# Sixty-six small transfers of a decoder step's output stage issued from GpSimd in place of SyncE

## The chip, the core and the metric

The kernel runs on one core of one Trainium2 chip. The metric is the time of one execution in device microseconds, as the median of several runs. A core has five engines with an instruction queue each: TensorE (PE in the profile, with its weight loads as PEld), VectorE (DVE), ScalarE (ACT), GpSimd (POOL) and SyncE (SP). Each works through its queue in order and waits on semaphores. SyncE computes nothing here; it only issues transfers. GpSimd computes and can issue transfers too. The transfers themselves run on 16 DMA engines that all queues share.

## What is computed

One inference step of one layer, for a prompt of 256 tokens and a sample of 8 sequences with 4 new tokens each (32 rows), with a width of 2048:

```
proj = x @ w_in                                  # 288 rows in all
y_r, s_T, new_shift = rwkv_time_mix(proj[..., :RWKV_COLS], ...)     # 16 heads, matrix state
y_n, ...            = nsa_mix(proj[..., RWKV_COLS:], ...)           # compressed, selected, window branch
h = concat([y_r, y_n]) @ w_out
x = layer_norm(ALPHA * x + h, ln1_g, ln1_b)
f = peer_ffn(x, ...)        # top-16 experts per head by product keys, rows of u and v gathered
x = layer_norm(ALPHA * x + f, ln2_g, ln2_b)
```

`new_shift` is the last projected row of the prompt and of each of the 8 sequences, 3360 columns each. The outputs are the two x, the new keys and values, the new states and these nine shift rows.

## The kernel before

The kernel is one long program written in stages; a scheduler puts the instructions of each engine in an order, by its own estimate of when each can start, among the instructions of several generators that are woven together. Which instruction stands where on an engine is therefore the scheduler's result, and a changed line can move others.

The stages in the order of time are: projection and recurrence of the prompt (up to line 1560), the sample's attention and recurrence (line 1578, `weave((late, 137), ...)`), the output stage (lines 1683 to 1688), layer norm 1 (lines 1695 to 1714), the product-key search (lines 1779 to 1805), the dense expert products (lines 1818 to 1845), and the sum over expert values with the last layer norm.

The change lies in the output stage. Three generators are woven there:

- `sample_chain` (line 1447) does the sample's 32 rows: it loads the gate weights (`gate_rows`, lines 1413 and 1414, into the ring `cw` of 5 buffers), multiplies (lines 1454 to 1456), and then forms the 32 rows times `w_out` in `product_rows`. Each of its 32 loads of 512 KB (line 1476, ring `cw`) feeds 4 matmuls (line 1478). `product_rows` takes them in two halves `h`, and four groups of four loads in a half; the first two groups multiply `YNs`, the others `BV`. After a group `put1` adds the sum on DVE: line 1486 for the first group of a half, which reads the input rows `xr_`, line 1488 for the others. Then come the norm with `gs_` and `bs_` (`norm_quarters`, lines 1436 and 1437), the same product with `peer_wq`, the choice of experts, and 64 gathers of rows of `peer_u` with a dot product each (lines 1533 and 1534).
- `prompt_attention` does the prompt's attention: lines 643 to 666 the compressed branch, lines 681 to 716 scores, exponentials, transposes (line 700) and value products (line 707).
- `out_first` (line 1660) transposes the shift rows (line 1666), copies them to the tile `SHR` (line 1667), stores them with 18 transfers (lines 1670 and 1671), computes the prompt's gate (lines 1677 to 1679, 8 pairs of matmuls from a second copy of the gate weights) and starts `out_part(0, BV)`: the prompt rows times the upper half of `w_out`, 16 loads of 512 KB (line 1642), each split into a rounded part on ACT (line 1644) and a rest on DVE or, for every fourth load, on GpSimd (line 1645), then 12 matmuls (line 1650). The buffers of line 1642 come from a ring `wraw` of 4, and `SHR` takes one of these four first, the gate weights two more.

The transfers that the change touches are those of lines 1464 and 1466 (in the generator `sample_chain`) and of lines 1670 and 1671. Lines 1464 and 1466 load `xr_` (for each half and quarter 4 loads of 8 rows by 256 columns, 32 in all) and `gs_` and `bs_` (8 loads each of one stretch of 256 numbers repeated over 32 rows). That is 32 + 16 + 18 = 66 transfers.

## Time and profile before

| | us |
|---|---|
| median of 3 runs | 2595.13 |
| lowest and highest of these | 2588.27 and 2599.22 |
| the profiled execution | 2602.22 |
| its span, first to last instruction | 2600.4 |
| PE busy / DVE busy / POOL busy in the span | 2328.9 / 1955.5 / 1281.1 |
| mean granted TensorE clock | 0.93 |

The profile is one execution. A row of its table of stretches gives for each engine the busy time and, after x, the number of instructions, then the granted clock of TensorE as a share of full speed (PEclk), then the share of the DMA engines that is busy and the rate. A row of its timeline gives the start, the time, the engine, the line, the operation, the tile written and the tiles read, a count, and in square brackets the idle time ahead of it with what ended it. SPq rows are the issues on SyncE's queue. A fp32 matmul shows as two records, a transpose as one, so that four matmuls of line 1478 are 8 records. In a timeline row that merges several records the time runs from the first start to the last end.

### The profile page before, as it was taken

To read this page: it belongs to the slowest core of one execution; us is meant where nothing else is said; L and a number is where in the kernel's file an instruction comes from. 1 tells how busy PE (TensorE), PEld (TensorE's weight loads), DVE (VectorE), ACT (ScalarE), POOL (GpSimd) and SP (SyncE) were. 2 spreads that over 40 slices of the span, in tenths; PEclk is the share of its full clock that TensorE was granted. 3 is DMA by queue.
4 is the path that set the end of the run, shared out by engine and by line. 5 is a ranking of instruction groups with operands and counts; after the bars stand their busy time and mean duration, and the time that the engine had idled before them with its cause. 6 is when DMAs were issued, how large, how long until landed. Compare 5 with 4: busy or idle time off the path is not lost.

```text
span 2600.4 us, 47649 instructions
## 1 busy us (share of the span) xinstructions
PE 2328.9 (90%) x17612; PEld 1961.5 (75%) x17612; DVE 1955.5 (75%) x4360; ACT 1027.7 (40%) x1932; POOL 1281.1 (49%) x1327
## 2 busy tenths in 40 slices
PE   7989999979989997469799999996699799989996
PEld 7877898865555655358699999995677688878885
DVE  4789756554742538949988888889976689878988
ACT  3433222224432332210244444443566544434443
POOL 5677423232510107635544444445555577767772
PEclk9989999988986997779899999997899999999998
DMA  7877964467656867886499999997778699899994
GB/s 222 241 218 241 275 199 139 130 200 223 213 178 234 275 243 245 312 267 172 153 371 349 352 352 346 352 338 225 232 241 294 233 324 326 319 336 322 325 322 174
DMA packets 346650, 683.49 MB, mean 263 GB/s; under 512 B 81338, under 2 KB 204785, under 8 KB 345361
## 3 DMA queue, kind: packets, MB, share of 16 engines
q1 hardware_dynamic: 251505, 344.67, 40.9%
q0 software_dynamic: 94912, 335.77, 36.9%
q8 instruction: 139, 2.28, 0.3%
q14 instruction: 94, 0.77, 0.1%
HBM read 664.77 MB, written 23.88 MB: 265 GB/s over the span
## 4 chain that ended last, share of the span: by engine, by line
PE 66%; DVE 17%; DMA 8%; issue 4%; POOL 3%; ACT 2%; SPq 0%; DVEq 0%; POOLq 0%; ACTq 0%
PE pb L2024 19%; PE ph L1832 14%; PE pj L417 6%; PE pt L1826 4%; DMA co<-in_cache_cmp_kv,gidx 2%; PE pj L1790 2%; PE pa L1650 2%; DVE rows L1756 2%; DVE CA L471 2%; PE ss L1478 2%; PE sa L918 1%; PE pa L1906 1%; PE p L1061 1%; PE px L1876 1%; PE fs L1924 1%
## 5 line engine op out<-in xcount | busy, mean ns | idle before, releaser
L448 POOL DMA_INDIRECT rq<-in_peer_v,gi x256 | 374.7, 1463 | 170.4 <-issue 80.7
L448 POOL DMA_INDIRECT rows<-in_peer_u,gi x256 | 298.6, 1166 | 313.3 <-DVE rows L1756 282.8
L1832 PE MATMUL ph<-XHd,ul 128*128 128x256 f32 x1024 | 304.6, 297 | 18.1 <-DVE ul L1622 18.1
L1756 DVE SCALAR_TENSOR_TENSOR rows<-rows,x1a 128x1024 f32<-128x1024 f32 x256 | 309.3, 1231 | 5.7 <-DMA rows<-in_peer_u,gi 5.5
L1832 PE MATMUL ph<-XHd,uh 128*128 128x256 f32 x1024 | 297.4, 290 | 0.3 <-ACT uh L1621 0.3
L1832 PE MATMUL ph<-XLd,uh 128*128 128x256 f32 x1024 | 290.7, 284 | 0.0
L1621 ACT CAST uh<-pt 128x512 fp32r<-128x512 f32 x256 | 149.8, 587 | 277.6 <-PE ph L1832 203.6
L417 PE MATMUL pj<-XH,wh 128*128 128x288 f32 (+1 forms) x752 | 230.4, 307 | 12.3 <-DVE ss L747 7.0
L417 PE MATMUL pj<-XH,wl 128*128 128x288 f32 (+1 forms) x752 | 232.2, 309 | 9.3 <-DVE wl L412 6.5
L1622 DVE TENSOR_TENSOR ul<-pt,uh 128x512 fp32r<-128x512 f32 x256 | 176.0, 689 | 80.8 <-ACT uh L1621 72.9
L417 PE MATMUL pj<-XL,wh 128*128 128x288 f32 (+1 forms) x752 | 226.7, 302 | 0.0
L2024 PE MATMUL pb<-vl,ah 128*128 128x512 f32 x768 | 217.7, 392 | 0.3 <-DVE vl L2018 0.3
L2024 PE MATMUL pb<-vh,al 128*128 128x512 f32 x768 | 216.4, 390 | 0.0
L2024 PE MATMUL pb<-vh,ah 128*128 128x512 f32 x768 | 199.1, 395 | 16.3 <-ACT vh L2017 16.3
L1832 PEld LDWEIGHTS ph<-XHd,ul 128*128 128x128 f32 x1024 | 196.7, 192 | 20.2 <-DVE ul L1622 20.0
L410 ACT CAST wh<-wraw 128x512 fp32r<-128x512 f32 (+1 forms) x188 | 114.8, 616 | 234.7 <-PE pj L417 180.2
L1832 PEld LDWEIGHTS ph<-XHd,uh 128*128 128x128 f32 x1024 | 197.3, 193 | 0.8 <-ACT uh L1621 0.5
L1832 PEld LDWEIGHTS ph<-XLd,uh 128*128 128x128 f32 x1024 | 197.0, 192 | 0.0
L1998 DVE SCALAR_TENSOR_TENSOR fP<-rq,ge,fP 128x512 f32<-128x512 f32 x254 | 189.9, 748 | 2.4
L2024 PEld LDWEIGHTS pb<-vh,ah 128*128 128x128 f32 x768 | 146.3, 191 | 47.7 <-ACT vh L2017 17.3
L471 DVE SCALAR_TENSOR_TENSOR CA<-co,wbc,CA 128x256 f32<-128x256 f32 x248 | 131.8, 570 | 55.8 <-DMA co<-in_cache_cmp_kv,gidx 55.6
L2024 PEld LDWEIGHTS pb<-vl,ah 128*128 128x128 f32 x768 | 145.8, 190 | 31.3 <-DVE vl L2018 0.7
(852 smaller groups left out, 5546.6 us busy)
## 6 DMA issues: line engine op xcount, KB each, us to landing
ur<-in_peer_u SPq DMA_DIRECT2D x128, 512.0 KB
wraw<-in_w_in SPq DMA_DIRECT2D x152, 256.0 KB
cw<-in_w_out SPq DMA_DIRECT2D x32, 512.0 KB
wraw<-in_w_out SPq DMA_DIRECT2D x32, 512.0 KB
cw<-in_peer_wq SPq DMA_DIRECT2D x32, 512.0 KB
wraw<-in_peer_wq SPq DMA_DIRECT2D x32, 512.0 KB
wraw<-in_w_in SPq DMA_DIRECT2D x64, 128.0 KB
co<-in_state_win_kv SPq DMA_DIRECT2D x16, 512.0 KB
```

Source lines behind the costliest of these rows:

```text
L410: sc.copy(wh[:, :, :n], w[:, :, :n])
L417: last[2] = pe.matmul(pb[:n, :nt], wi[:, k, :n], xi[(o + k) // 8][:, (o + k) % 8, :nt], start=(o + k == 0 and wi is wh and xi is xh), stop ...
L448: gp.indirect_dma_start(out=dst, out_offset=None, in_=rows_, in_offset=bass.IndirectOffsetOnAxis(ap=ix, axis=0))
L471: ve.scalar_tensor_tensor(d_, x_, w_, d_, op0=OP.mult, op1=OP.add)
L1478: pe.matmul(pb[32 * q:32 * q + 32, :256], lhs(k), w[:, 256 * q:256 * q + 256], start=(k % 4 == 0), stop=(k % 4 == 3))
L1621: sc.copy(xh, pb)
L1622: return ve.tensor_tensor(xl, pb, xh.bitcast(F32), OP.subtract)
L1756: i_ = ve.scalar_tensor_tensor(r_, r_, 1.0, X1a[t], op0=OP.mult, op1=OP.mult, accum_out=h_)
L1826: pe.transpose(pb[:, 128 * e:128 * e + 128], w[:, 512 * q + 128 * e:512 * q + 128 * e + 128], ident)
L1832: mm = pe.matmul(ph[:, :NPR], wi[:, e, :], xi[:, 4 * q + e, :NPR], start=(q == 0 and e == 0 and wi is wh and xi is XHd), stop=(q == 1 and ...
L1998: ve.scalar_tensor_tensor(fP[t], r_, w_, fP[t], op0=OP.mult, op1=OP.add)
L2024: pe.matmul(acc[3 * t + q], wi[:, P * t:P * t + P], xi[:, 512 * q:512 * q + 512], start=(k == 0 and wi is ah and xi is vh), stop=(k == P - ...
```

## The change

The 66 transfers are issued by GpSimd (`gp`) in place of SyncE (`sy`). Nothing else is changed in the source.

```diff
             for q in range(4):
                 c_, l_ = cols(h, q)
                 for i in range(4):
-                    sy.dma_start(xr_[32 * q + 8 * i:32 * q + 8 * i + 8, l_], a["x_sample"][:, i, c_])
+                    gp.dma_start(xr_[32 * q + 8 * i:32 * q + 8 * i + 8, l_], a["x_sample"][:, i, c_])
                 for t_, nm in ((gs_, "ln1_g"), (bs_, "ln1_b")):
-                    sy.dma_start(t_[32 * q:32 * q + 32, l_], bass.AP(
+                    gp.dma_start(t_[32 * q:32 * q + 32, l_], bass.AP(
                         tensor=a[nm].tensor, offset=a[nm].offset + c_.start, ap=[[0, 32], [1, 256]]))
...
         for i in range(9):
             r_, o_ = SHR[27 * (i % 4):27 * (i % 4) + 27, i // 4, :], outs[11][0, i - 1, 0] if i else outs[6][0, 0, 0]
-            sy.dma_start(o_[:3328].rearrange("(b c) -> b c", c=P), r_[:26])
-            sy.dma_start(o_[3328:].rearrange("(b c) -> b c", b=1), r_[26:27, 64:96])
+            gp.dma_start(o_[:3328].rearrange("(b c) -> b c", c=P), r_[:26])
+            gp.dma_start(o_[3328:].rearrange("(b c) -> b c", b=1), r_[26:27, 64:96])
```

The scheduler then also sets other instructions of the output stage in another order. Below, `cw` and `wraw` are the two rings named above. On SyncE, before the change, the last of the 66 transfers and the first weight loads of the stage stand in this order; 64 more of the 66 stand between the second `L1414 DMA cw` of the stage and this place:

```order
L1466 DMA gs__10162<-in_ln_g 32x256
L1466 DMA bs__10163<-in_ln_b 32x256
L1476 DMA cw<-in_w_out 128x1024 x4
L1413 DMA wraw<-in_rwkv_g 128x1024
L1414 DMA wraw<-in_rwkv_g 32x1024
L1476 DMA cw<-in_w_out 128x1024
L1642 DMA wraw<-in_w_out 128x2x512
```

After the change the weight loads stand directly behind `L1414 DMA cw`:

```order
L1414 DMA cw<-in_rwkv_g 32x1024
L1476 DMA cw<-in_w_out 128x1024 x3
L1413 DMA wraw<-in_rwkv_g 128x1024
L1414 DMA wraw<-in_rwkv_g 32x1024
L1642 DMA wraw<-in_w_out 128x2x512
L1476 DMA cw<-in_w_out 128x1024 x5
L1642 DMA wraw<-in_w_out 128x2x512
```

The first load of `w_out` has moved up by 66 places, and the second and third loads of line 1642 now come among the first eight of line 1476. On GpSimd the 66 transfers now stand between the last gather of the sample's attention and its first subtraction of line 1645, in this order: 14 of lines 1464 and 1466, the 18 of lines 1670 and 1671, and 34 of lines 1464 and 1466.

On TensorE, behind the last transpose of the shift rows, stands before the change (sa, pb and sao are PSUM banks of the prompt's attention):

```order
L1666 MATMUL pa<-CT_61,SHO 27x128
L643 MATMUL sa<-cb_89,QT 128x8 x16
L659 MATMUL sa<-CT_61,Sc 128x128
L665 MATMUL sa<-VcB,PcT 128x512 x2
L681 MATMUL sa<-KT,QT 128x128 x10
L700 MATMUL pb<-CT_61,Sm 128x128 x2
L681 MATMUL sa<-KT,QT 128x128 x2
```

and after it (ss is the bank of the sample's product, pa that of the gate):

```order
L1666 MATMUL pa<-CT_61,SHO 27x128
L1478 MATMUL ss<-cw,YNs 32x256 x12
L643 MATMUL sa<-cb_89,QT 128x8 x8
L1478 MATMUL ss<-cw,YNs 32x256 x4
L643 MATMUL sa<-cb_89,QT 128x8 x8
L1677 MATMUL pa<-sg_102,wraw 128x256
L1678 MATMUL pa<-sg_103,wraw 128x256
```

Matmuls of the sample's product and of the gate have moved ahead of most of the first attention block. Up to the first matmul of line 1650 the new order holds 32 matmuls of line 1478, 16 of line 643, 8 of each of lines 1677 and 1678, one of line 659, two of line 665 and 8 of line 681. The old order holds there all of these and, besides, 29 more of line 1478, 12 more of line 681 and 14 each of lines 700 and 707. On DVE the first line 1486 stands before the change behind four blocks of score maxima (line 690), with the first two lines 1645 behind it; after the change it stands behind two such blocks, with two lines 1645 ahead of it and the third four rows behind it. At the last matmul of the sample's second product (lines 1476 to 1478 with `peer_wq`) both orders have done the same matmuls of all lines but for 8 transposes and value products.

## Prediction and its working, ahead of the result

> **What bounds the kernel now.** I looked first at the table of stretches around the output stage, then at SyncE's timeline there, then at TensorE's rows. Stretches, in us from the start of the span:

> ```profile
> core 0: us, PE busy (x) PEld busy (x) DVE busy (x) ACT busy (x) POOL busy (x), PEclk, DMA share, GB/s
> 760.00:774.00 14.00, 12.06 (x43) 9.52 (x43) 4.16 (x18) 0.98 (x4) 0.00 (x0) 0.50 0.09 23
> 774.00:797.00 23.00, 17.96 (x85) 12.85 (x85) 6.00 (x33) 5.50 (x23) 0.00 (x0) 0.57 0.30 77
> 797.00:831.00 34.00, 33.81 (x153) 15.87 (x152) 11.61 (x36) 8.36 (x24) 0.00 (x0) 0.50 0.81 280
> 831.00:836.00 5.00, 5.00 (x40) 2.59 (x38) 1.96 (x4) 0.62 (x1) 0.00 (x0) 0.94 0.67 196
> 836.00:940.00 104.00, 103.73 (x704) 67.50 (x703) 47.69 (x132) 38.07 (x90) 9.51 (x4) 0.98 0.88 300
> 940.00:970.00 30.00, 27.42 (x210) 16.34 (x206) 10.47 (x49) 12.21 (x41) 0.00 (x0) 0.89 0.54 187
> 970.00:1140.00 170.00, 92.53 (x397) 71.03 (x394) 144.63 (x301) 42.35 (x72) 106.30 (x88) 0.70 0.81 280
> ```

> Between 760 and 797 the DMA engines are nearly empty (0.09 and 0.30) while TensorE idles for 5.0 of the last 23 us and works at about half clock. From 797 to 940 TensorE is the bound: busy 142.5 of 143 us, the first 34 of them at a clock of 0.50. From 970 on DVE, gathers and DMA carry the stage. SyncE shows why the loads come late:

> ```profile
> 761.59 0.34 SPq L1414 DMA_DIRECT2D cw<-in_rwkv_g  x1
> 762.02 0.62 SPq L1464 DMA_DIRECT2D xr__10161<-in_x_sample  x2
> 763.16 0.32 SPq L1670 DMA_DIRECT2D out<-wraw  x1
> ...
> 774.29 0.31 SPq L1670 DMA_DIRECT2D out<-wraw  x1
> ...
> 792.23 0.42 SPq L1466 DMA_DIRECT2D bs__10163<-in_ln_b  x1
> 792.74 1.79 SPq L1476 DMA_DIRECT2D cw<-in_w_out  x4
> ```

> From 762.02 to 792.65 SyncE issues the 66 small transfers (including a wait for the third copy of line 1667), and the first load of `w_out` follows at 792.74. It is used 4.4 us later:

> ```profile
> 773.90 3.59 PE L643 MATMUL sa<-cb,QT 64*128 64x8 f32 x32
> ...
> 797.10 1.08 PE L1478 MATMUL ss<-cw,YNs 128*32 128x256 f32 x8
> ...
> 835.71 0.50 PE L1650 MATMUL pa<-wh,YH 128*128 128x512 f32 x1
> ```

> **What the change does on SyncE and TensorE.** The weight loads move from 792.74 to about 762.0, some 30.7 us earlier. That is not the gain, since TensorE had work in most of that time. Its work comes next. Busy time by kind in 773 to 831:

> ```profile
> L681 PE MATMUL sa<-KT,QT 64*128 64x128 f32 x40 | 8.4, 379 | 1.1 <-DVE m L687 0.8
> L1478 PE MATMUL ss<-cw,YNs 128*32 128x256 f32 x64 | 8.2, 634 | 0.0
> L1678 PE MATMUL pa<-sg,wraw 32*128 32x256 f32 x12 | 7.3, 709 | 0.0
> L1677 PE MATMUL pa<-sg,wraw 128*128 128x256 f32 x12 | 7.3, 710 | 0.0
> ...
> L643 PE MATMUL sa<-cb,QT 64*128 64x8 f32 x32 | 3.6, 359 | 0.0
> L665 PE MATMUL sa<-VcB,PcT 128*128 128x512 f32 x4 | 3.6, 1047 | 0.4 <-ACT PcT L661 0.4
> ...
> L659 PE MATMUL sa<-CT,Sc 128*128 128x128 f32 x1 | 0.4, 445 | 2.3 <-DVE Sc L655 2.3
> ```

> In the new order the first line 1650 needs ahead of it, at these half-clock prices: 64 records of line 1478, 8.2 us; lines 1677 and 1678, 32 records for the 24 shown, 19.5; line 643, 3.6; line 665, 3.6; line 659, 0.4; 16 of the 40 records of line 681, 3.4. Together 38.7 us. Begun at 773.9, where the gate's matmuls of the sample end in both orders, this ends at 812.6, if nothing has to wait. TensorE has other work wherever it idled, so I cost its idle time at nothing; the loads that this work needs are at hand by 12 us (three of `cw`) or arrive in the 4.4 us shown, while 3.6 us of line 643 stand between.

> The whole work of 774 to 836 is, in microseconds at full clock, 17.96 x 0.57 + 33.81 x 0.50 + 5.00 x 0.94 = 10.2 + 16.9 + 4.7 = 31.8. The 38.7 us are 19.4 of these; 12.4 remain. If TensorE runs at half clock up to the first line 1650 and at full clock behind it, the work takes 38.7 + 12.4 = 51.1 us in place of 62: 10.9 us gained, of which 5.0 are the idle time and the rest is the clock. The 0.57 of the second stretch holds 0.07 x 23 / 0.5 = 3.2 us at full clock, around the four records of line 665, the densest in it. In the new order line 665 stands among line 1677, which leaves at least that burst: it adds about 3.2 us. **I take 14 us.** The ends: 5 us, if only the idle time goes and the clock rises as late in the work as now; 30 us (62 less 31.8), if the clock is full from 774 on. I take 14 because line 1650 is the first kind of work at which the trace holds a clock of 0.98 for long (836 to 940).

> Full occupation alone does not raise the clock here: TensorE is busy 33.81 of 34 us at 0.50. [...]

> What follows keeps the gain. Up to 940 TensorE is the bound, and at the last matmul of the second sample product both orders have done the same work but for 8 small matmuls. Then the choice of experts starts the gathers, and the chain of waits behind goes through them:

> ```profile
> by line: DVE cw L1534 17.4%; DMA cw<-in_peer_u,gi 12.8%; DMA wraw<-in_peer_wq 12.7%; issue 12.2%; DVE wl L1645 4.8%; PE pj L1790 4.5%; POOL cw L448 4.4%; PE pa L1650 3.7%; DVE lnst L1610 2.7%; DVE x L1658 2.4%; PE sa L681 2.2%; DVE x L1616
> ```

> (960 to 1140). None of it waits for anything but this stage, so it shifts whole.

> **What the change adds on GpSimd.** Its timeline has 22 plain transfers, all at the start, and then shows the free time here:

> ```profile
> 1.32 1.28 POOL L349 DMA_DIRECT2D shA<-in_state_shift  x2 [0.31 <-issue]
> ...
> 6.79 0.51 POOL L333 DMA_DIRECT2D prow<-in_rwkv_k_a  x1 [0.77 <-DMA shA<-in_state_shift]
> ...
> 12.91 0.50 POOL L333 DMA_DIRECT2D prow<-in_rwkv_r_k  x1 [2.71 <-DMA pgi<-in_page_table]
> ...
> 17.76 1.59 POOL L349 DMA_DIRECT2D shA<-in_state_shift  x3 [0.15 <-issue]
> ...
> 733.55 0.93 POOL L448 DMA_INDIRECT co<-in_cache_sel_kv,sidx  x1 [0.30 <-PE st L960]
> 844.00 2.38 POOL L1645 TENSOR_TENSOR wl<-wraw,wh 128x1024 fp32r<-128x1024 f32 x1 [109.52 <-PE pb L700]
> ```

> GpSimd is idle from 734.5 to 844, so the 66 issues collide with no compute of its own; behind them waits its first line 1645. A transfer costs 0.51 us to issue, and the ninth waits for the first to land (it was issued by 2.0 and released the ninth at 6.79, 5 us later): eight are in flight. The 22 went in 1.32 to 19.35, 18.0 us, 0.82 us each under a DMA load. I take 0.82; the bounds are 0.51 (no wait) and 1.7 (the four from 6.0 to 12.91, held up by the small pieces of the page table). [...]

> At 0.82 from 762.5 on:
> - `xr_` of the first half is complete with the 40th issue: 762.5 + 32.8 + 5 = 800. DVE needs it in line 1486, which stands behind the maxima of the 8th line 681, so at about 812. Cover 12 us. Without it DVE waits, and behind it the third line 1645.
> - The 18 stores are issues 15 to 32, landed by 762.5 + 26.2 + 5 = 794. The fourth load of line 1642 takes over their buffer; if it has to wait, SyncE's queue stands with all later loads. TensorE needs it at about 828: 812.6, plus 36 matmuls of line 1650 at the 0.246 of the row below, 8.9, plus 20 of line 1478 at half the price above, 2.6, plus an estimated 4 us of attention. Cover some 25 us, with the 4.4 us of a load taken off.
> - The 66th issue ends at 762.5 + 54.1 = 816.6, and GpSimd's line 1645 of 2.38 us at 819, needed at the same 828. Cover 9 us; it is gone at (828 - 2.4 - 762.5) / 66 = 0.96 us each.
> - `gs_`, `bs_` and the second half of `xr_` are needed later than all this; they cost nothing.

> From the chain of waits, 12 matmuls of line 1650 at full clock:

> ```profile
> 840.08 2.95 PE pa L1650 x12
> ```

> So the sum is a gain of 14 us and no cost: 2602.2 - 14 = 2588 for an execution like the profiled one. That one lies 7.1 us above the median of 2595.13; from the median the forecast is **2581 us**.

> **The rivals.**
> 1. The clock rises early: the new order has no idle stretch from 764 on, and full-array matmuls (lines 1677 and 665) come sooner. For it speaks the burst at line 665; against it the 34 busy microseconds at 0.50, with many of line 1677 in them. It gains 20 to 30 us; taken as 26, 2569 us. [...]
> 2. The gain is eaten. Transfers of GpSimd at 1.2 us each, as the gathers were issued in this very stage:

> ```profile
> 991.15 0.97 POOL L448 DMA_INDIRECT cw<-in_peer_u,ig  x1 [3.43 <-DVE ig L1529]
> ...
> 999.56 1.80 POOL L448 DMA_INDIRECT cw<-in_peer_u,ig  x1 [0.80 <-issue]
> ```

> (7 issues in 8.4 us), end at 762.5 + 79.2 = 841.7, line 1645 at 844, 16 us late against a gain of 14: 2597 us. The same result comes if the clock stays low into line 1650 and small waits take the 5 us of idle time.
> 3. Slower: GpSimd's queue becomes the bound of the stage. The mechanism is the eight in flight with weight loads filling the DMA engines (0.81 in 797 to 831) from 762 on. Past 0.96 us each, every 0.1 us costs 6.6 us in TensorE's wait for GpSimd's line 1645; at 1.17 the gain is gone, from 1.37 the kernel is slower by over 13 us. At 1.4: 762.5 + 92.4 + 2.4 = 857, 29 late, 15 lost, 2610 us. For it speak the 1.7 us stretch and the 5 us landing; against it the larger cover at 0.82 and that the page-table pieces made that stretch long.

> That the loads don't come earlier is excluded by the order of SyncE.

> **How the numbers follow.** Forecast (gain 8 to 20): 0.46. Rival 1: 0.17. Rival 2: 0.22. Rival 3: 0.15. 0.5% is 13 us, about what a measurement of this kernel can tell from no change. The forecast lies past it in about three of five cases, 0.28; with rival 1, faster 0.45. Same: 0.18 + 0.22 = 0.40. Slower 0.15. The range reaches from 2562 (most of rival 1) to 2607 (rival 2 and the beginning of rival 3); the forecast's own is 2575 to 2587.

> **What the profile after would show.** Right: SyncE issues line 1476 at about 762; line 1478 starts near 774; the first line 1650 near 813 with the clock rising there; no idle time of DVE ahead of line 1486; GpSimd's line 1645 waiting for ACT and not for its queue; the stage past 836 some 14 us earlier, and so to the end. Wrong: TensorE's first line 1650 waiting for line 1645 of GpSimd, SyncE standing at line 1642 for the stores (rivals 2 and 3), a clock near 1.0 before line 1650 (rival 1), or a gain at 836 that is lost again by 1140.

## The result, and the profile after

The changed kernel takes 2580.98 us (median of 10 executions, 2571.74 to 2589.34), the kernel before on the same chip 2595.41 us (10 executions). The ratio is 0.9943, with a 95% interval of 0.9924 to 0.9962. A second comparison on another chip (below) gave 0.9964, 0.9943 to 0.9986. So the change makes the kernel faster by some 9 to 14 us, and the forecast was 14.

The profiled execution of the changed kernel has a span of 2570.0 us. It can't be laid over that of before as it stands: its output stage begins 9 us earlier (first record of line 1454 at 755.65, before at 764.7), and nothing ahead of that was changed. In a second profile of each kernel the first line 1454 stands at 764.9 (changed) and 751.8 (before), so this start varies by some 13 us from execution to execution. From here on, times with a plus or minus sign are counted from the first record of line 1454 in the same execution.

The table of stretches of the changed kernel, with the bounds of the prediction's table (which therefore lie 9 us later in its stage):

```profile
core 0: us, PE busy (x) PEld busy (x) DVE busy (x) ACT busy (x) POOL busy (x), PEclk, DMA share, GB/s
760.00:774.00 14.00, 13.06 (x87) 8.84 (x87) 3.55 (x12) 1.51 (x3) 8.83 (x18) 0.62 0.89 261
774.00:797.00 23.00, 22.68 (x110) 12.48 (x110) 11.30 (x38) 7.91 (x24) 13.72 (x27) 0.90 0.80 259
797.00:831.00 34.00, 29.93 (x240) 19.09 (x240) 11.77 (x52) 12.16 (x44) 2.46 (x1) 0.88 0.81 294
831.00:836.00 5.00, 5.00 (x45) 3.37 (x44) 2.66 (x4) 1.42 (x2) 0.00 (x0) 0.77 0.05 8
836.00:940.00 104.00, 102.11 (x764) 68.48 (x763) 45.05 (x153) 42.59 (x109) 7.12 (x3) 0.98 0.78 265
```

The DMA engines are now busy (0.89 and 0.80 where 0.09 and 0.30 stood), TensorE idles for 0.3 us instead of 5.0 in the second row, and its clock there is 0.90 instead of 0.57. In the third row it idles for 4.1 us, which it did not do before.

SyncE's timeline shows the loads moved up, and a gap:

```profile
752.55 0.34 SPq L1414 DMA_DIRECT2D cw<-in_rwkv_g  x1
752.98 1.32 SPq L1476 DMA_DIRECT2D cw<-in_w_out  x3
...
764.05 4.14 SPq L1476 DMA_DIRECT2D cw<-in_w_out  x5
...
783.10 7.34 SPq L1642 DMA_DIRECT2D wraw<-in_w_out  x3
799.39 0.34 SPq L1476 DMA_DIRECT2D cw<-in_w_out  x1
```

The first load of line 1476 is issued at -2.7, before it was at +28.0. From 790.4 to 799.4 SyncE issues nothing: the next load wants a buffer of the ring `cw`, and the matmuls that free it stand on TensorE behind 24 of line 1650.

TensorE's timeline, and then rows of the table of stretches with its clock:

```profile
764.85 2.79 PE L1478 MATMUL ss<-cw,YNs 128*32 128x256 f32 x24
...
771.52 0.95 PE L1677 MATMUL pa<-sg,wraw 128*128 128x256 f32 x2
...
775.85 3.28 PE L1478 MATMUL ss<-cw,YNs 128*32 128x256 f32 x26
...
790.62 0.50 PE L1650 MATMUL pa<-wh,YH 128*128 128x512 f32 x1
```

```profile
769.00:770.00 1.00, 0.06 (x6) 0.04 (x6) 0.00 (x0) 0.00 (x0) 0.00 (x0) 1.00 1.00 389
...
772.00:773.00 1.00, 1.00 (x4) 0.50 (x2) 0.69 (x4) 0.21 (x1) 0.25 (x1) 0.50 1.03 333
777.00:778.00 1.00, 1.00 (x14) 0.41 (x9) 0.00 (x0) 0.00 (x0) 0.52 (x1) 0.50 0.84 205
778.00:779.00 1.00, 1.00 (x10) 0.34 (x2) 0.00 (x0) 0.36 (x1) 0.64 (x2) 0.67 0.68 209
779.00:780.00 1.00, 1.00 (x5) 0.61 (x5) 0.28 (x1) 0.68 (x1) 0.99 (x3) 1.00 0.90 335
...
822.00:833.00 11.00, 10.58 (x40) 7.64 (x41) 4.67 (x25) 4.04 (x18) 0.00 (x0) 0.55 0.51 185
```

The clock is full for a moment at 769 and again from 779 on, 12 us ahead of the first line 1650, and that one comes at +35.0 (before +71.0). The last row lies behind SyncE's gap, and the two may belong together. From 755 to 940 TensorE waits for loads of line 1476

```profile
PE ss L1478 <- DMA cw<-in_w_out: 3.7, 5, 1.3
```

(total, times, longest). The first of the five waits is the 0.94 us at 769; the other four, 2.7 us, end between 807 and 814. The clock stays full behind them and falls only at 823.0, right behind a wait of 1.20 us for DVE (line 681, from 821.2), for 10 us. That the gap set off this fall is not shown.

GpSimd's timeline:

```profile
740.00 2.14 POOL L1464 DMA_DIRECT2D xr__10161<-in_x_sample  x4 [14.67 <-ACT kt L919]
...
761.23 0.52 POOL L1670 DMA_DIRECT2D out<-wraw  x1 [2.85 <-DMA out<-wraw]
...
791.04 0.52 POOL L1466 DMA_DIRECT2D bs__10163<-in_ln_b  x1
798.30 2.46 POOL L1645 TENSOR_TENSOR wl<-wraw,wh 128x1024 fp32r<-128x1024 f32 x1 [6.75 <-ACT wh L1644]
```

From 745.94 to 791.56 it issues 62 transfers, 0.74 us each; it waits for landings now and then (2.85 us for the first of eight), and its line 1645 waits for ACT, not for its own queue.

### The profile page after: what moved, and what is told of

Its sections match the earlier page's. It is cut to its first block, busy times and chain, and to the rows that moved or that the text cites. A ratio compares the mean times of both kernels' runs of the same rounds, so it can differ in the third digit from the quotient of the medians.

```text
span 2570.0 us, 47676 instructions
## 1 busy us (share of the span) xinstructions
PE 2308.4 (90%) x17612; PEld 1951.9 (76%) x17612; DVE 1952.9 (76%) x4360; ACT 1027.3 (40%) x1932; POOL 1316.9 (51%) x1393
## 4 chain that ended last, share of the span: by engine, by line
PE 68%; DVE 14%; DMA 8%; issue 5%; POOL 3%; ACT 2%; SPq 0%; DVEq 0%; POOLq 0%; ACTq 0%
PE pb L2024 20%; PE ph L1832 13%; PE pj L417 8%; PE pt L1826 4%; PE pa L1650 2%; DMA co<-in_cache_cmp_kv,gidx 2%; PE p L1061 2%; DVE rows L1756 2%; PE pj L1790 2%; PE pa L1906 2%; PE sa L918 2%; PE fs L1924 1%; PE px L1876 1%; DVE CA L471 1%; PE sc L937 1%
## 5 line engine op out<-in xcount | busy, mean ns | idle before, releaser
L448 POOL DMA_INDIRECT rq<-in_peer_v,gi x256 | 374.7, 1464 | 170.1 <-DVE fP L1998 75.6
L448 POOL DMA_INDIRECT rows<-in_peer_u,gi x256 | 298.9, 1168 | 311.4 <-DVE rows L1756 276.8
L1832 PE MATMUL ph<-XHd,ul 128*128 128x256 f32 x1024 | 304.8, 298 | 16.6 <-DVE ul L1622 16.6
L1621 ACT CAST uh<-pt 128x512 fp32r<-128x512 f32 x256 | 149.8, 587 | 276.7 <-PE ph L1832 213.1
L1832 PEld LDWEIGHTS ph<-XHd,uh 128*128 128x128 f32 x1024 | 197.2, 193 | 0.9 <-ACT uh L1621 0.5
L2024 PEld LDWEIGHTS pb<-vl,ah 128*128 128x128 f32 x768 | 145.3, 189 | 30.6 <-DVE vl L2018 0.2
```

What stands on the lines that cost most here:

```text
L448: gp.indirect_dma_start(out=dst, out_offset=None, in_=rows_, in_offset=bass.IndirectOffsetOnAxis(ap=ix, axis=0))
L1621: sc.copy(xh, pb)
L1832: mm = pe.matmul(ph[:, :NPR], wi[:, e, :], xi[:, 4 * q + e, :NPR], start=(q == 0 and e == 0 and wi is wh and xi is XHd), stop=(q == 1 and ...
L2024: pe.matmul(acc[3 * t + q], wi[:, P * t:P * t + P], xi[:, 512 * q:512 * q + 512], start=(k == 0 and wi is ah and xi is vh), stop=(k == P - ...
```

## Two paths to the end

To compare kernels I read five places in each trace: the first and the last line 1478 (the last ends the sample's second product), the first gather of `peer_u`, the first and the last line 1790 (the product-key search of the prompt), and the span. The dense expert products begin right behind the last line 1790 and take nearly the same time everywhere: from it to the end are 1348 to 1357 us in all runs. The places are those of one execution each, and an execution can lie far from its median: that of stores_only lies 18 us above, that of changed 9 us below, the others up to 7 us to either side. Ratios are against the kernel before on the same chip.

| kernel | first 1478 | last 1478 | first gather | first 1790 | last 1790 | end | ratio (95%) |
|---|---|---|---|---|---|---|---|
| before | +32.4 | +200.9 | +218.9 | +367.3 | +486.0 | +1835.7 | 1 |
| before_again | +34.0 | +193.5 | +211.6 | +360.1 | +481.1 | +1829.3 | 0.9996 (0.9967–1.0025) |
| changed | +9.2 | +177.5 | +202.2 | +344.2 | +463.9 | +1814.3 | 0.9943 (0.9924–0.9962) |
| after_again | +9.2 | +176.3 | +201.0 | +340.8 | +462.3 | +1815.4 | 0.9964 (0.9943–0.9986) |
| loads_only | +9.2 | +182.3 | +199.2 | +356.5 | +475.5 | +1823.4 | 0.9973 (0.9952–0.9994) |
| stores_only | +22.7 | +213.1 | +233.7 | +344.9 | +495.9 | +1852.8 | 1.0023 (1.0002–1.0044) |
| merged_on_sync | +23.6 | +200.5 | +219.5 | +342.7 | +484.8 | +1836.0 | 1.0046 (1.0023–1.0070) |
| all_on_act | +9.2 | +190.4 | +207.3 | +373.7 | +491.9 | +1842.7 | 1.0066 (1.0042–1.0090) |
| late_on_sync | +9.2 | +194.2 | +218.9 | +346.0 | +478.6 | +1829.8 | 0.9979 (0.9963–0.9995) |
| no_small | +9.2 | +181.3 | +199.4 | +361.3 | +480.4 | +1828.1 | 0.9967 (0.9944–0.9989) |
| split_on_gpsimd | +9.2 | +227.9 | +255.6 | +351.1 | +513.5 | +1864.7 | 1.0107 (1.0084–1.0130) |
| order_of_before | +31.7 | +185.9 | +207.9 | +322.9 | +475.9 | +1825.6 | 0.9995 (0.9970–1.0020) |
| six_buffers | +9.2 | +179.7 | +203.2 | +345.3 | +464.8 | +1813.1 | 0.9930 (0.9906–0.9953) |
| merged_on_gpsimd | +9.9 | +175.5 | +195.5 | +349.5 | +468.2 | +1816.7 | 0.9924 (0.9897–0.9951) |

The last line 1790 follows from two paths. Where the prompt's path decides, it comes 118 to 122 us behind the first line 1790. Where the sample's path decides, it comes some 261 us behind the first gather. Take the later of "first 1790 plus 119" and "first gather plus 261": that gives the last line 1790 within 5 us in thirteen of the fourteen rows (order_of_before is 7 later). Before, the two lay close together: 486.3 and 479.9, in the second profile 479.1 and 472.6. In the changed kernel both came down, to 463.2 each. This sum, with its two constants, is a fit to these same rows and not an independent test; the places are measured.

## The experiments

Formed before the first runs: theory T, the gain is SyncE's freed queue; the rivals are named in each expectation. Line numbers are those of the kernel before.

**stores_only**: the diff's last two lines alone (lines 1670 and 1671 to `gp`).

> Only the 18 shift-row stores (lines 1670 and 1671) go to GpSimd, the 48 loads stay on SyncE. In SyncE's order the weight loads of line 1476 then stand behind 48 small transfers in place of 66. Theory T (the gain comes from the weight loads being issued earlier, and is spent on TensorE's idle and half-clock time): 48 issues at the 0.46 us that SyncE took before (30.6 us for 66) are 22 us, so line 1476 comes some 8 us earlier than before; of the 5.0 us of idle time most goes, the clock hardly rises earlier: 3 to 6 us faster than before, ratio 0.9977 to 0.9988. Rival S (the stores are what matters, since they wait for ScalarE's copies on SyncE): nearly the full gain, 12 to 16 us, ratio 0.994 to 0.995. Rival G (the gain is all or nothing, it needs the loads of line 1476 ahead of the first attention block): no change, 0 +- 2 us.

Measured: 1.0023, 4 us slower by the medians, with an interval that hardly excludes no change. SyncE's loads came 10 us earlier and the first line 1478 too (+22.7), but the sample's second product ended 12 us later than in the first profile of before. Loads that come earlier are no gain by themselves; T is wrong in this form, and so is rival S; rival G's no change is the nearest.

**loads_only**: the diff's first two lines alone (lines 1464 and 1466 to `gp`).

> Only the 48 loads (lines 1464 and 1466) go to GpSimd, the 18 stores stay on SyncE, where two loads of line 1476 now stand ahead of them and the rest behind. Theory T: two weight loads come 30 us earlier and the others behind the last store, which waits for the third copy of line 1667, at about 774 of the frame of before in place of 793, so 18 us earlier: most of the gain, 8 to 14 us, ratio 0.9946 to 0.997. Rival S (the stores are what matters): 0 to 4 us. Rival G (all or nothing): 12 to 16 us, since TensorE's order has line 1478 and the gate ahead of the attention as in the changed kernel.

Measured: 0.9973, about 6.5 us faster by the medians. T's range ended at 0.997 (8 us): just short of it. S (0 to 4) and G (12 to 16) fail too. SyncE had only two weight loads ahead of the 18 stores here, and TensorE waited 3.0 us for one of the next.

**merged_on_sync**:

```diff
-                for i in range(4):
-                    sy.dma_start(xr_[32 * q + 8 * i:32 * q + 8 * i + 8, l_], a["x_sample"][:, i, c_])
+                sy.dma_start(xr_[32 * q:32 * q + 32, l_], bass.AP(
+                    tensor=a["x_sample"].tensor, offset=a["x_sample"].offset + c_.start, ap=[[2048, 4], [8192, 8], [1, 256]]))
...
+                sy.dma_start(t_[:, 256 * h:256 * h + 256], bass.AP(
+                    tensor=a[nm].tensor, offset=a[nm].offset + 1024 * h, ap=[[256, 4], [0, 32], [1, 256]]))
```

> All transfers stay on SyncE, but the 32 loads of line 1464 are merged into 8 and the 16 of line 1466 into 4 (same bytes, same destination), so that 30 small transfers stand ahead of line 1476 in place of 66. Theory T: 36 issues fewer at 0.46 us are 16.6 us; line 1476 is issued some 16 us earlier, without GpSimd in it: 6 to 12 us faster, ratio 0.9954 to 0.9977. Rival P (the path over GpSimd is what helps): 0 us. Rival O (the order that the scheduler gives TensorE, with line 1478 and the gate ahead of line 643 to 681, is what helps; here TensorE keeps the attention first): 0 to 5 us although the loads come earlier.

Measured: slower, 1.0046, though the first line 1478 came 9 to 10 us earlier. T had 6 to 12 us of gain here and fails. Rival O named the reason, the order, but allowed no loss. The stretch shows why the gain is missing:

```profile
786.50:813.50 27.00, 27.00 (x89) 13.88 (x88) 8.61 (x20) 6.77 (x17) 0.00 (x0) 0.50 0.54 180
```

TensorE has its loads, never idles, and still works at 0.50 for 27 us: here too the scheduler put the attention first, and the clock rose only at +66. Why the kernel is slower than before, and not equal, is open: its places are those of the first profile of before.

**all_on_act**: the 66 transfers by `sc` in place of `gp`.

> All 66 transfers are issued by ScalarE in place of GpSimd; SyncE is as free as in the changed kernel. Theory T (the gain is SyncE's, the engine that takes the issues matters only by what stands behind them): SyncE's weight loads come as early as in the changed kernel, and ScalarE, which before was busy 14 of the 57 us from 774 to 831, takes some 30 us of issues on top; exponentials, transposes' copies and the roundings of line 1644 stand behind these, so a part of the gain is lost: between 5 us slower and 12 us faster than before, the weight loads early and TensorE waiting for ACT. Rival P (GpSimd's own path of transfers is what helps): 10 us slower or more. If ScalarE's issues are as free as GpSimd's: 14 us faster, ratio 0.9943.

Measured: 1.0066, 15 us slower, beyond T's 5 and in the range of rival P. SyncE and the first line 1478 (+9.2) are as in the changed kernel, so the loss is not SyncE's. ScalarE's own work stood behind the issues (ScalarE's timeline):

```profile
815.93 0.20 ACT L636 COPY Gt<-sa 128x48 f32<-128x48 f32 x1 [51.10 <-DMA xr__10161<-in_x_sample]
```

It computed nothing for 51.1 us. What stands behind the issues on their engine is the likely price of the move, and GpSimd had nothing there; P itself is tested below (late_on_sync).

After these four I replaced T by T2, a theory that the gain is decided by TensorE's order and clock up to the end of the sample's second product, and the early loads are only a condition.

**after_again**: the changed kernel, unchanged.

> The changed kernel once more, beside the others on the same chip, for its ratio there and a second profile. It was 14.4 us below the kernel before; expected 10 to 18 us, ratio 0.993 to 0.996. In the profile, from the first matmul of line 1454: the last matmul of line 1478 (the end of the sample's second product) some 178 us later, as in the first profile (before: 201), within 5 us.

Measured: 0.9964, 9 us by the medians, a little less than expected; the places of the profile agree with the first within 4 us.

**late_on_sync**: all stays on SyncE, later in the source; `after()` issues the 48 loads.

```diff
+                    if after and h == 0 and kb == 1:
+                        after()
                     put(h, kb == 2, pb[:, :256])
+                    if after and kb == 1:
+                        x_ = x1s[:, 256 * h:256 * h + 256]
+                        ve.scalar_tensor_tensor(x_, xr_[:, 256 * h:256 * h + 256], ALPHA, x_, op0=OP.mult, op1=OP.add)
...
             if first:
-                ve.scalar_tensor_tensor(x_, xr_[:, 256 * h:256 * h + 256], ALPHA, pb, op0=OP.mult, op1=OP.add)
+                ve.tensor_copy(x_, pb)
```

> All 66 transfers stay on SyncE, but stand later in the source: the 48 loads behind the third group of four weight loads of the first half, the 18 stores behind the loads of the prompt's gate weights. So that the input rows may come later, they are added behind the fourth group of a half instead of with the first (one more DVE operation in each half, about 0.3 us). TensorE's order then begins as in the changed kernel (12 matmuls of line 1478 behind the last shift-row transpose). Theory T2, formed after the first four runs (the gain is decided by TensorE's order and clock up to the end of the sample's second product, for which the early weight loads are needed, not GpSimd): 6 to 16 us faster, ratio 0.994 to 0.9977, the last line 1478 at about +180 to +188 us from the first line 1454. Rival P (GpSimd's queue is needed, SyncE pays for every one of its 66 issues wherever they stand): 0 or slower, since 66 x 0.46 = 30 us of issues still lie between the weight loads.

Measured: 0.9979 (0.9963 to 0.9995), about 5 us, just short of T2's range. So GpSimd isn't needed for a gain, against rival P; but the issues still lie between the weight loads, TensorE waits 6.1 us for line 1476 and 7.6 for the loads of `peer_wq`, and the last line 1478 comes at +194, later than T2 said.

**no_small**: the three tiles are set by `gp.memset`, the loop of lines 1670 and 1671 is left out.

> The 66 small transfers are left out: the sample's input rows, its norm's scale and shift are set to 1 by three GpSimd instructions, and the nine shift rows are not stored. Bounds what the 66 transfers still cost the changed kernel on GpSimd. Theory T2: nothing but a few us; 12 to 18 us faster than before, the same as the changed kernel within 4 us. Rival C (on GpSimd they still cost, by the DMA queues, late xr_ or the held buffer of SHR): 20 us faster or more.

Measured: 0.9967, the same as the changed kernel beside it (0.9964). So no cost of the 66 transfers on GpSimd can be measured, against rival C; but the kernel is only some 8 us faster than before, below T2's 12 to 18. The two kernels also differ in order (first line 1790 at +361 and +341), so a small cost could be hidden in that.

**split_on_gpsimd**: each of the 48 loads in two halves.

```diff
+                    for z in range(2):
+                        gp.dma_start(xr_[32 * q + 8 * i:32 * q + 8 * i + 8, 256 * h + 128 * z:256 * h + 128 * z + 128], a["x_sample"][:, i, c_.start + 128 * z:c_.start + 128 * z + 128])
```

> The changed kernel with each of the 48 loads split in two halves of 128 columns (same bytes): 114 transfers on GpSimd in place of 66. At the 0.74 us each that the changed kernel shows (62 issues in 45.6 us) they end some 36 us later, at about +72 us from the first line 1454 where the changed kernel's end at +36; GpSimd's first line 1645 then comes some 29 us later than it did. Rival 3 of the prediction (past its cover GpSimd's queue holds up TensorE one for one): the gain of 14 is lost and more, 5 to 20 us slower than before. Theory T2 (TensorE has other work to do meanwhile, ordered by the scheduler; what counts is the end of the sample's second product): between 5 us slower and 10 us faster, TensorE waiting for POOL's line 1645 by less than 15 us.

Measured: 1.0107, 27 us slower: worse than rival 3 had it. The queue was late as expected (GpSimd's and SyncE's timelines):

```profile
818.58 2.56 POOL L1465 DMA_DIRECT2D xr__10161<-in_x_sample  x5 [2.19 <-issue]
...
829.24 2.37 POOL L1647 TENSOR_TENSOR wl<-wraw,wh 128x1024 fp32r<-128x1024 f32 x1
```

```profile
790.14 16.59 SPq L1644 DMA_DIRECT2D wraw<-in_w_out  x4
829.18 27.50 SPq L1478 DMA_DIRECT2D cw<-in_w_out  x16
```

(These lines 1465, 1647, 1644 and 1478 are 1464, 1645, 1642 and 1476 of the kernel before.) But no matmul waits for POOL up to 960. The scheduler, which foresaw the longer queue, set line 1650 and the attention ahead of the sample's next matmuls; these come only at 828.04, until then no buffer of `cw` is freed, SyncE stands for 22.4 us, and the DMA engines fall to a share of 0.15 (the last column but one of this row of the table of stretches).

```profile
807.00:830.00 23.00, 18.35 (x100) 13.88 (x102) 7.34 (x41) 8.12 (x31) 20.21 (x40) 0.68 0.15 39
```

Whether the queue alone, with the order of the changed kernel, would have cost as much is open.

**before_again**: the kernel before, unchanged.

> The kernel before once more, for a second profile of it and for the spread of a ratio that should be 1: within 0.998 to 1.002. In the profile, from the first matmul of line 1454: the last line 1478 at +201, the first matmul of line 1832 (start of the dense expert products) at +488, as in the first profile, within 5 us. If these come earlier by 8 us or more, the first profile of before was an unusual one and the change gains less than the two profiles show.

Measured: 0.9996 (0.9967 to 1.0025), as it should be. Its places from the last line 1478 on lie 5 to 7 us earlier than in the first profile, a little outside the 5 expected; between the means of the two profiles each the change gains 17.7 us at the end, where the medians give 14.4 and 9.

**order_of_before**: the changed kernel, and TensorE held to the old order; `hold[7]` is the 8th transpose of line 700.

```diff
-    weave((take(chain, 38), 38), (prompt_attention(), 19), (out_first(), 19))
+    pat = prompt_attention()
+    weave((take(pat, 4), 4))
+    weave((take(chain, 38), 38), (pat, 15), (out_first(), 19))
...
+                        with tc.issue_after(hold[7].ins):
                             for q in range(4):
                                 pe.matmul(pb[32 * q:32 * q + 32, :256], lhs(k), w[:, 256 * q:256 * q + 256],
...
+            with tc.issue_after(hold[7].ins):
                 pe.matmul(pb[:, :NPR], g2a[:, 128 * j:128 * j + 128], sg0[:, :NPR], start=True, stop=False)
```

> The changed kernel (66 transfers on GpSimd, weight loads early on SyncE), but TensorE's order is held as in the kernel before: the matmuls of lines 1478 and 1677 and 1678 may only be issued behind the 8th transpose of line 700, so that the first block of the prompt's attention stands ahead of them. Theory T2 (the order of TensorE's work decides; early loads are only its condition): the gain is lost, between 4 us faster and 8 us slower than before, the last line 1478 (here line 1481) at +190 or later. Theory T (SyncE's freed queue and the early weight loads are the gain, TensorE takes its work in either order): 9 to 14 us faster, since no load is waited for.

Measured: 0.9995 (0.9970 to 1.0020): no gain is left that can be measured, as T2 said and T did not. The interval lies outside that of the first comparison of the changed kernel and overlaps that of the second (0.9943 to 0.9986). But the gain did not go where I expected it to: the last line 1478 is not late (+190 or later), it comes at +185.9. The first 80 us behind the first line 1454 (columns as in the table of stretches), in before_again,

```profile
751.80:831.80 80.00, 74.88 (x389) 46.76 (x389) 23.65 (x78) 18.30 (x54) 2.39 (x1) 0.67 0.65 217
```

in the changed kernel,

```profile
755.60:835.60 80.00, 74.68 (x493) 47.46 (x492) 30.08 (x105) 23.37 (x74) 27.79 (x51) 0.81 0.78 262
```

and in order_of_before:

```profile
755.10:835.10 80.00, 74.68 (x471) 47.31 (x471) 30.47 (x105) 23.54 (x75) 27.62 (x51) 0.81 0.74 237
```

TensorE's clock is as good as in the changed kernel, with the first attention block ahead again. Over these 80 us it is 0.59 to 0.67 in the four profiles with late loads (before, before_again, stores_only, merged_on_sync) and 0.75 to 0.84 in nine of the ten whose first load of line 1476 is issued at about -3. The tenth is all_on_act, with 0.61, so early loads are not enough by themselves. In order_of_before TensorE spent the clock on the prompt: the first line 1790 comes at +322.9, 21 us ahead of the changed kernel, while the sample's product ends 9 us behind it, at +185.9. The chain that ended last runs, ahead of the last matmuls of line 1790 (here line 1796), through the sample's gathers,

```profile
1104.40 7.91 DMA cw<-in_peer_u,gi
1113.90 6.85 DMA cw<-in_peer_u,ig
1124.83 10.20 PE pj L1796 x32
```

and in the changed kernel through the prompt's weights:

```profile
1075.38 12.89 DMA wraw<-in_peer_subkeys
1088.27 21.15 DMA wraw<-in_peer_wq
```

The prompt's 21 us are of no use while the sample's path is behind. So T2 is right that the order counts, and T had a part: where the loads come early the clock is mostly higher, and the order decides which path gets it. Since this kernel's order is the old one only at its beginning, and its profiled execution does end 7 us earlier than the mean of the two of before, how much of the gain the order carries is not shown.

**six_buffers**: `NCW = 6` in the changed kernel.

> The changed kernel with six buffers in the ring cw in place of five. In the changed kernel SyncE stands 9 us for a free buffer of cw (from +34.8 to +43.8 after the first line 1454) and TensorE then waits 3.7 us for loads of line 1476 and falls to half clock for some 8 to 11 us. If this stall costs what it seems (3.7 us of waiting and about 4 us by the clock): 5 to 8 us faster than the changed kernel, 15 to 20 faster than before. If the stall is hidden or the order that the scheduler then makes is another: the same as the changed kernel within 4 us, or slower.

Measured: 0.9930 (0.9906 to 0.9953), 16.9 us faster than before by the medians. The waits for line 1476 fell from 3.7 to 1.3 us, but the last line 1478 stands at +179.7, no earlier. Its interval overlaps those of the changed kernel; that the stall costs anything in the end is not shown.

**merged_on_gpsimd**: the diff of merged_on_sync with `gp`.

> The changed kernel with the 32 loads of line 1464 merged into 8 and the 16 of line 1466 into 4 (same bytes), so that GpSimd issues 30 transfers in place of 66. GpSimd's queue then ends some 27 us earlier. Theory T2: GpSimd's issues were hidden in the changed kernel (its line 1645 waited 6.75 us for ACT, not for its queue), so the same as the changed kernel, 8 to 15 us faster than before. If GpSimd's issues cost something there: over 16 us faster.

Measured: 0.9924 (0.9897 to 0.9951), the lowest ratio of all runs, by less than the intervals can tell from the changed kernel's 0.9943. By the medians it is 14.6 us faster than before, within T2's 8 to 15; by the ratio it is some 20 us, past the 16 at which GpSimd's issues would have a cost. So this run does not decide between the two. The same merge on SyncE was slower than before: the two ratios, each against the kernel before on its own chip, differ by 1.2%.

## Why the prediction was right, and where it was not

**Loads earlier by 30.7 us; line 1478 at the end of the gate's matmuls.** Right: +28.0 became -2.6, and +32.4 became +9.2 (the forecast's 773.9).

**The clock rises at the first line 1650.** This step failed. Line 1650 was forecast for 812.6, which is +47.9, and came at +35.0: the work that was priced at 38.7 us took 25.8. The clock was full 12 us before it, and in the kernel before's second profile the rise stands at +52, 14 us ahead of line 1650 (+66), where the first has it at +67:

```profile
802.80:803.80 1.00, 1.00 (x10) 0.20 (x8) 0.00 (x0) 0.37 (x1) 0.00 (x0) 0.50 0.72 180
804.80:805.80 1.00, 1.00 (x4) 0.39 (x3) 0.42 (x1) 0.00 (x0) 0.00 (x0) 1.00 0.92 342
```

In merged_on_sync and stores_only it came 1 to 2 us behind the first line 1650. So line 1650 is not the trigger. Nor is line 665, for which the forecast added 3.2 us: in the second profile of before it passes without a burst, and the changed kernel has one at 768.4, ahead of its line 665. An early rise is the mechanism of rival 1, to which I gave 0.17; its 20 to 30 us in the stage are nearly what the profiles show up to the last line 1478 (the two means: 197.2 against 176.9, 20.3 us).

**What follows keeps the gain.** Right in size, wrong in reason. Between the means of two profiles each, the first gather comes 13.7 us earlier (215.3 and 201.6) and the end 17.7. But I took the chain behind for one that waits for this stage alone. There are two paths, within 7 us of each other before, and a gain on one of them alone counts for little: order_of_before had 40 us on the prompt's path (+322.9 against +363.7) and no gain in time that can be measured.

**No cost.** SyncE's gap from 790.4, the 3.7 us of waiting (2.7 of them behind the gap) and the 11 us at 0.55 (10.58 x 0.45 = 4.8 us lost) were not in the sum. They stand inside the 20.3 us, which would have been more without them. At the end the profiles show 17.7, and the medians 14.4 and 9. Why these are lower is not shown, but executions of one kernel lie up to 18 us apart in the first comparison alone. So it is partly luck that a forecast of 14 us, with the wrong moment for the clock and no cost, came out near the measured number.

**GpSimd's cover.** Right: 0.74 us for each transfer (taken: 0.82, and gone at 0.96), no wait of line 1645 for the queue, 0.2 us of DVE for `xr_` at line 1486, and no_small no faster. The queue was done at +35.9, where the forecast had +51.9, mainly because GpSimd began at -15.7, ahead of this stage, and not at -2.2. Rival 2 did not occur.

**Rival 3.** Its point was tested with 114 transfers. The sign is right and the size beyond it (27 us against 5 to 20), but TensorE did not wait for GpSimd; the loss came by the order that the scheduler made of the longer queue and by the ring `cw`.

## What to carry to other kernels

Moving issues off a full queue paid here where the engine that took them had nothing waiting behind them (GpSimd: no cost measured; ScalarE: 51 us of standstill) and where the freed time reached both paths that end together. Where a scheduler sets the order, compare orders before costing waits: early loads gave 0.994 and 0.9995 with two orders of TensorE. And find the second-latest path before forecasting that a gain goes through to the end.

## What the runs showed of the hardware

What sets the moment is left open: in the profiles of before, before_again, changed, six_buffers, merged_on_gpsimd and split_on_gpsimd a rise came 3 to 5 us behind four matmuls of lines 1677 and 1678 in a row (3.9 and 3.5 us in the two of before, 2.7 in that of changed). But in the first profile of before two such groups (from 807 and from 815) passed without one, and in order_of_before the clock rose at 789.7, ahead of the first of them at 790.56. A stop of 0.94 us at 769 was followed by 6.8 us at half clock (771.8 to 778.7 in the changed kernel), at which TensorE does 3.4 us less work than at full clock. If the stop is the cause, which only the order in time speaks for, that is more than three times the wait itself.
